# Where the low halves of two weight units are summed: VectorE or an accumulating DMA

## The chip, the cores and the metric

The kernel runs on one core of a Trainium2 chip. The metric is the device time of one execution in microseconds (us); the time given for a kernel is the median of its runs. A profile is one more execution, taken with the hardware profiler; its span runs from the first to the last instruction.

## The reference

Two layers of a transformer-like trunk are run for 640 tokens (128 context tokens and 512 latent tokens) with 1024 features, all in float32. Each layer has a mixer (a recurrent unit, neighbourhood attention, differential attention) and then a channel mixer, which is where the change lies:

```python
def conv_ffn(h, p):
    u = dwconv_centred(h @ p['ffn_up'], p['ffn_conv_w'], p['ffn_conv_b'])
    val, gate = jnp.split(u, 2, axis=-1)
    return (jax.nn.gelu(gate) * val) @ p['ffn_down']
```

`ffn_up` is 1024 x 5632 and `ffn_down` 2816 x 1024 in each layer; the 2816 middle features are handled as 22 tiles of 128, each with a value half and a gate half.

## The kernel before, in words

**Three products for one.** A float32 operand is held as a high half in the fast type fp32r and a low half, the rest. A product is formed as high x high + low x high + high x low, three matrix instructions for each. The split of a weight unit is made by `unit` (L366): ScalarE copies the source into the high half (`wh`, through `copy`, L110), and VectorE subtracts that from the source into the low half (`wl`, through `sub`, L117). Both halves live in a ring of four buffers of 128 x 1024 elements for each half.

**Seven products for eight.** For tiles 3 to 21 of the 22, class `Up` forms the 2 x 2 block product of weights and tokens with seven products (Strassen and Winograd's scheme) in place of eight. `up_weights` (L552) prepares the weights of one tile: two DMAs on SyncE's queue load them (`up_load`, L549), VectorE writes a sum `s1` (L556, tile `pT`) and an edit of the first half of the loaded buffer in place; then come unit y (first half of the buffer), unit x (second half, as loaded), two more in-place edits, which overwrite the second half, unit z (the edited second half) and a small unit `ws`, split from `s1`. y, x and z have 128 x 1024 elements each. Every edit and split is on VectorE or ScalarE; GpSimd does nothing in this stage.

**Order of the work.** One pass of the loop in `ffn` handles one tile. TensorE's products for the tile, in the order of the trace and in its names: p2 (`s<-h`, unit x), part of a `ffn_down` product (`m<-act`, unit of `rawd`), p4 (`t<-tx`, x), p6 (`m<-tx`, z), then p1 of the next tile (`m<-h`, y), p5 (`m<-h,ws`), p7 of the next tile (`t<-tx`, y), p3 (`m<-h`, z), and three more `ffn_down` parts (`s<-act`, `m<-act`, `s<-act`). Each is 12 matrix instructions on 320 columns. The order in which each engine's instructions stand is fixed ahead of time by a planner, which takes the ready instruction of the best priority by its own estimates of durations; it can set a matrix instruction ahead of another that it expects to wait. On the chip each engine runs its list in that order and waits where an operand is late. A ring buffer goes to whichever unit comes next when it falls free.

p6, p5 and p3 are added into one PSUM bank in turn, with a copy out by ScalarE (`raw<-m`, `u<-m`) between them: p5 may not start before the copy behind p6 is done.

Of the kernel before, what the change touches and what calls it, by code (L numbers as in the profile page):

```python
# [10 lines left out]
F32 = mybir.dt.float32  # L11
FR = mybir.dt.float32r
I32 = mybir.dt.int32
AF = mybir.ActivationFunctionType
OP = mybir.AluOpType
# [53 lines left out]
def trunk_kernel(ctx: ExitStack, tc: tile.TileContext, A, O):  # L69
    nc = tc.nc  # L70
# [19 lines left out]
    def pT_tile(w):  # L90
        return gen.tile([P, T], F32, tag="pT", name="pT", bufs=2)[:, :w]
# [16 lines left out]
    def copy(eng, out, in_):  # L108
        if eng == "a":
            return nc.scalar.activation(out, in_, AF.Copy)  # L110
        elif eng == "v":
            nc.vector.tensor_copy(out, in_)
        else:
            nc.gpsimd.tensor_copy(out, in_)

    def sub(out, a, b, eng=None):
        (eng or nc.vector).tensor_tensor(out, a, b, op=OP.subtract)  # L117
# [35 lines left out]
    for t in range(NT):  # L153
        src = A["x_prompt"] if t == 0 else A["x_sample"]
# [211 lines left out]
    split = []  # L366

    def unit(src, k, eng="a", home=None):
        wh, wl = [home(f"w{x}") if home else ring.tile([P, 1024], FR, tag=f"w{x}", name=f"w{x}") for x in "hl"]
        n = int(np.prod(src.shape[1:]))  # L370
        wh, wl = [w[:, :n].rearrange("p (k c) -> p k c", k=k) for w in (wh, wl)]
        split.append(copy(eng, wh, src))
        sub(wl, src, wh.bitcast(F32))
        return wh, wl

    def lx_groups(h, units, *jh):
# [33 lines left out]
    with tc.tile_pool(name="pro", bufs=1) as pro:  # L410
        raws = lx_load(0, [0])
        units = [unit(raws[j], 8) for j in range(2)]
        ws = [pro.tile([P, 2048], F32, name=f"pro{k}") for k in range(KD - 1)]
        ws = [[w[:, i * 512:i * 512 + 512] for i in range(4)] for w in ws]
# [30 lines left out]
        for part in range(4):  # L445
# [8 lines left out]
            if part < 3:  # L454
                for hf in range(2):
                    norm_apply(xt, 0, 0, hf + 2, h, range(part * 2 + 2, part * 2 + 4))
        units.append(unit(raws[2], 8))

    def attn_consts(l, mix):
# [33 lines left out]
    def wsplit(raw, nk, ncol, by_k=False, home=None):  # L493
        raw = raw[:, :nk * ncol].rearrange("p (k c) -> p k c", k=nk)
        kk, cc = (nk // 2, ncol) if by_k else (nk, ncol // 2)
        parts = [unit(raw[:, i * kk:i * kk + kk] if by_k else raw[:, :, i * cc:i * cc + cc], kk, home=home)
                 for i in range(2)]

        def get(k, c0, c1):
            i = k // kk if by_k else c0 // cc  # L500
            k, o = (k - i * kk, 0) if by_k else (k, i * cc)
            return tuple(w[:, k, c0 - o:c1 - o] for w in parts[i])
        return get
# [41 lines left out]
    def up_load(l, i):  # L545
        raw = raw_tile("up")
        w3 = raw.rearrange("p (k c) -> p k c", k=8)
        for v in range(2):
            nc.sync.dma_start(w3[:, :, v * P:v * P + P], dram(A["ffn_up"], l * D * 2 * FF + v * FF + i * P,  # L549
                                                            ((2 * FF, P), (P * 2 * FF, 8), (1, P))))  # L550
        return w3

    def up_weights(l, i):
        w3 = up_load(l, i)
        s1 = pT_tile(512).rearrange("p (k c) -> p k c", k=4)
        nc.vector.tensor_tensor(s1, w3[:, :4, P:], w3[:, 4:, P:], op=OP.add)  # L556
        yield
        sub(w3[:, :4, P:], w3[:, :4, :P], w3[:, :4, P:])
        y = unit(w3[:, :4], 4)
        yield y  # L560
        x = unit(w3[:, 4:], 4)
        yield x
        sub(w3[:, 4:, P:], s1, w3[:, :4, :P])
        sub(w3[:, 4:, :P], w3[:, 4:, :P], w3[:, 4:, P:])
        z = unit(w3[:, 4:], 4)
        yield z
        w = ring.tile([P, 1024], FR, tag="ws", name="ws", bufs=1)
        wh, wl = [w[:, i:i + 512].rearrange("p (k c) -> p k c", k=4) for i in (0, 512)]
        copy("a", wh, s1)
        sub(wl, s1, wh.bitcast(F32))  # L570
        yield wh, wl

    def up_begin(l, i):
        g = up_weights(l, i)
        next(g)
        return g, next(g), next(g)
# [923 lines left out]
```

## Time and profile before

| | us |
|---|---|
| median of 3 runs (1621.7 to 1622.51) | 1622.3 |
| the profiled execution | 1619.05 |
| its span, first to last instruction | 1616.9 |

Shares of the span in the profile are averages over many stages; the rows below take the stages apart. PE is TensorE's matrix instructions, PEld its weight loads, which overlap them; DVE is VectorE, ACT ScalarE, POOL GpSimd, SP SyncE. In a timeline row the first number is the start in us and the second the duration; a bracket holds the idle time of the engine just before, and what ended it. Matrix instructions are pipelined: one begins about every 0.147 us while its row says 0.31.

### The profile page before, as it was taken

The page shows a single profiled execution, that of the slowest core. Times are in us where ns is not written, and L with a number is a line of the kernel's source. Part 1 is how long each engine was busy: PE and PEld are TensorE (multiplying, and loading weights), DVE is VectorE, ACT ScalarE, POOL GpSimd, SP SyncE. Part 2 cuts the span into 40 slices and gives each one's busy share as a digit, 9 for nine tenths or more (in the row PEclk, how much of TensorE's full clock was granted, in tenths as well). Part 3 has the DMA queues.
Part 4 walks back from the last instruction along what each step waited for, and adds up shares of the span by engine and source line. Part 5 has one row for each costly group of instructions (what it writes and reads, how often), then busy time and mean ns, then how long its engine had stood idle before and what let it go on. Part 6 is the DMA issues. An engine that isn't in the chain of part 4 may idle for free.

```text
span 1616.9 us, 28663 instructions
## 1 busy us (share of the span) xinstructions
PE 1575.7 (97%) x11183; PEld 1466.1 (91%) x11183; DVE 1327.0 (82%) x2885; ACT 921.0 (57%) x1689; POOL 112.4 (7%) x98
## 2 busy tenths in 40 slices
PE   6999999999999999999999899999999999999998
PEld 5877688799999999999998777888999999999998
DVE  5886758888999888888897775778889998888884
ACT  5865647746655445445468656576475544544451
POOL 0310300102000000000012211000100000000000
PEclk8999999999999999999999999999999999999999
DMA  9566541131444333222244563221222332222221
GB/s 327 178 195 223 128 142 37 69 106 37 140 127 138 106 92 92 84 76 72 89 143 145 175 211 92 95 86 46 79 63 72 91 103 79 79 80 79 72 72 66
DMA packets 208070, 177.30 MB, mean 110 GB/s; under 512 B 47575, under 2 KB 197311, under 8 KB 201791
## 3 DMA queue, kind: packets, MB, share of 16 engines
q1 hardware_dynamic: 207934, 175.48, 35.3%
q8 instruction: 88, 1.44, 0.4%
q14 instruction: 48, 0.39, 0.1%
HBM read 165.12 MB, written 10.34 MB: 109 GB/s over the span
## 4 chain that ended last, share of the span: by engine, by line
PE 86%; DVE 6%; DMA 3%; ACT 2%; issue 2%; SPq 1%; POOL 0%; ACTq 0%; DVEq 0%; POOLq 0%
PE m L277 6%; PE m L279 6%; PE m L278 6%; PE m L1238 6%; PE m L1239 6%; PE m L1240 6%; PE s L278 4%; PE s L279 4%; PE s L277 4%; PE m L268 4%; PE m L270 4%; PE m L269 4%; PE t L1240 3%; PE t L1238 3%; PE t L1239 3%; PE t L934 2%
## 5 line engine op out<-in xcount | busy, mean ns | idle before, releaser
L117 DVE TENSOR_TENSOR wl<-up,wh 128x1024 fp32r<-128x1024 f32 x126 | 156.3, 1245 | 38.1 <-ACT wh L110 37.1
L1296 DVE SCALAR_TENSOR_TENSOR u<-raw,vec,u 128x127 f32<-128x127 f32 x352 | 175.8, 546 | 0.8 <-ACT u L1290 0.8
L110 ACT ACTIVATE wh<-up 128x1024 fp32r<-128x1024 f32 x126 | 132.2, 1051 | 77.7 <-PE t L1240 43.2
L268 PE MATMUL m<-wh,h 128*128 128x256 f32 x480 | 140.3, 292 | 0.0
L270 PE MATMUL m<-wh,h 128*128 128x256 f32 x480 | 138.3, 288 | 0.0
L269 PE MATMUL m<-wl,h 128*128 128x256 f32 x480 | 137.8, 287 | 0.0
L277 PE MATMUL m<-act,wh 128*128 128x320 f32 (+2 forms) x376 | 116.7, 311 | 0.0
L278 PE MATMUL m<-act,wl 128*128 128x320 f32 (+2 forms) x376 | 116.6, 310 | 0.0
L277 PE MATMUL s<-act,wh 128*128 128x320 f32 (+2 forms) x376 | 116.4, 310 | 0.0
L278 PE MATMUL s<-act,wl 128*128 128x320 f32 (+2 forms) x376 | 116.3, 309 | 0.0
L279 PE MATMUL s<-act,wh 128*128 128x320 f32 (+2 forms) x376 | 116.3, 309 | 0.0
L279 PE MATMUL m<-act,wh 128*128 128x320 f32 (+2 forms) x376 | 116.1, 310 | 0.0
L279 PE MATMUL m<-h,wh 128*128 128x320 f32 (+2 forms) x352 | 111.2, 319 | 3.0 <-DVE h L117 1.9
L277 PE MATMUL m<-h,wh 128*128 128x320 f32 (+2 forms) x352 | 112.5, 321 | 0.3 <-DVE xt L531 0.2
L278 PE MATMUL m<-h,wl 128*128 128x320 f32 (+2 forms) x352 | 111.3, 317 | 0.0
L531 DVE SCALAR_TENSOR_TENSOR xt<-m,mod,xt 128x128 f32<-128x128 f32 (+3 forms) x236 | 95.8, 432 | 14.2 <-PE m L279 13.1
L268 PEld LDWEIGHTS m<-wh,h 128*128 128x128 f32 x480 | 91.8, 191 | 14.5 <-issue 11.2
L269 PEld LDWEIGHTS m<-wl,h 128*128 128x128 f32 x480 | 91.9, 191 | 3.1 <-issue 2.9
L1238 PE MATMUL m<-h,wh 128*128 128x320 f32 x304 | 94.5, 311 | 0.0
L110 ACT ACTIVATE raw<-m 128x320 f32<-128x320 f32 x126 | 54.5, 432 | 70.1 <-PE m L1240 60.3
L270 PEld LDWEIGHTS m<-wh,h 128*128 128x128 f32 x480 | 91.7, 191 | 2.9 <-issue 2.4
L1240 PE MATMUL t<-tx,wh 128*128 128x320 f32 x304 | 94.2, 310 | 0.0
(364 smaller groups left out, 5072.1 us busy)
## 6 DMA issues: line engine op xcount, KB each, us to landing
up<-in_ffn_up_dram SPq DMA_DIRECT2D x88, 512.0 KB
adaw<-in_ada_w_dram SPq DMA_DIRECT2D x40, 1024.0 KB
w<-in_w_in_dram SPq DMA_DIRECT2D x16, 1024.0 KB
rawd<-in_ffn_down_dram SPq DMA_DIRECT2D x24, 512.0 KB
pro<-in_ada_w_dram SPq DMA_DIRECT2D x30, 256.0 KB
w<-in_w_out_dram SPq DMA_DIRECT2D x8, 768.0 KB
rawd<-in_ffn_down_dram SPq DMA_DIRECT2D x16, 384.0 KB
xd<-xt SPq DMA_DIRECT2D x4, 1280.0 KB
```

The costliest lines, as they stand in the source:

```text
L110: return nc.scalar.activation(out, in_, AF.Copy)
L117: (eng or nc.vector).tensor_tensor(out, a, b, op=OP.subtract)
L268: nc.tensor.matmul(out, st[0], mv[0], start=(i == 0), stop=False)
L269: nc.tensor.matmul(out, st[0], mv[1], start=False, stop=False)
L270: nc.tensor.matmul(out, st[1], mv[0], start=False, stop=(i == n - 1))
L277: nc.tensor.matmul(out, a[0], b[0], start=(k == total[0]), stop=False)
L278: nc.tensor.matmul(out, a[1], b[0], start=False, stop=False)
L279: last = nc.tensor.matmul(out, a[0], b[1], start=False, stop=(k == total[-1]))
L1238: nc.tensor.matmul(ps, st[0], mv[0], start=first and k == 0, stop=False, skip_group_check=chk)
L1239: nc.tensor.matmul(ps, st[1], mv[0], start=False, stop=False, skip_group_check=chk)
L1240: nc.tensor.matmul(ps, st[0], mv[1], start=False, stop=last and k == 3, skip_group_check=chk)
L1296: nc.vector.scalar_tensor_tensor(u[:, oa:ob], r[:, oa + sft:ob + sft], w, u[:, oa:ob], op0=OP.mult, op1=OP.add)
```

## The change

In `unit`, a new mode "d" has ScalarE write the high half as before, then a second ScalarE instruction writes the negated source, in fp32r, into the low half, and a DMA issued from GpSimd's queue adds the source onto it. `up_weights` uses the mode for y and x; z and `ws` stay as they are, and so do all units outside `up_weights`.

```diff
-        split.append(copy(eng, wh, src))
-        sub(wl, src, wh.bitcast(F32))
+        split.append(copy("a" if eng == "d" else eng, wh, src))
+        if eng == "d":
+            nc.scalar.activation(wl, src, AF.Copy, scale=-1.0)
+            nc.gpsimd.dma_start(wl, src, accum_op=OP.add)
+        else:
+            sub(wl, src, wh.bitcast(F32))
...
-        y = unit(w3[:, :4], 4)
+        y = unit(w3[:, :4], 4, "d")
         yield y
-        x = unit(w3[:, 4:], 4)
+        x = unit(w3[:, 4:], 4, "d")
         yield x
```

## Rows read from the trace of the kernel before

**Rows 1.** The page, part 1: busy us, share of span, instructions.
```profile
PE 1575.7 (97%) x11183; PEld 1466.1 (91%) x11183; DVE 1327.0 (82%) x2885; ACT 921.0 (57%) x1689; POOL 112.4 (7%) x98
```

**Rows 2.** Windows, both seven-product stages: us, busy by engine, clock, DMA share, GB/s.
```profile
424.00:800.00 376.00, 376.00 (x2563) 366.43 (x2562) 328.15 (x589) 189.69 (x280) 0.00 (x0) 1.00 0.35 104
...
1217.00:1576.00 359.00, 359.00 (x2444) 358.26 (x2444) 317.17 (x545) 183.53 (x274) 0.00 (x0) 1.00 0.28 82
```

**Rows 3.** Timeline of TensorE, one tile and the next.
```profile
567.51 0.31 PE L279 MATMUL s<-act,wh 128*128 128x320 f32 x1
...
574.69 0.31 PE L1238 MATMUL m<-h,wh 128*128 128x320 f32 x1
574.84 0.31 PE L1239 MATMUL m<-h,wl 128*128 128x320 f32 x1
...
576.45 0.31 PE L1238 MATMUL m<-h,ws 128*128 128x320 f32 x1
...
587.16 0.31 PE L1239 MATMUL s<-h,wl 128*128 128x320 f32 x1
...
593.76 0.31 PE L1239 MATMUL m<-h,wl 128*128 128x320 f32 x1
```

**Rows 4.** Waits of TensorE's weight loads, 1217 to 1576: us, times, longest.
```profile
PEld m L1238 <- ACT raw L110: 0.4, 2, 0.2
PEld m L278 <- DVE wl L117: 0.2, 1, 0.2
```

**Rows 5.** Tile `pT` (the sum `s1`): its instructions; what VectorE waited for.
```profile
L556 DVE TENSOR_TENSOR pT<-up x38: 682/686/962, 384.4 to 1527.9; 128x512 f32<-128x512 f32 x38
...
  DMA up<-in_ffn_up_dram: 3.7, 7
```

**Rows 6.** Groups of VectorE, 1217 to 1576.
```profile
L117 DVE TENSOR_TENSOR wl<-up,wh 128x1024 fp32r<-128x1024 f32 x55 | 67.1, 1224 | 20.3 <-ACT wh L110 20.0
```

**Rows 7.** The page, part 5: ScalarE's copies of weight units.
```profile
L110 ACT ACTIVATE wh<-up 128x1024 fp32r<-128x1024 f32 x126 | 132.2, 1051 | 77.7 <-PE t L1240 43.2
```

**Rows 8.** Windows of 1 us, end of one tile's weight loads.
```profile
588.00:589.00 1.00, 1.00 (x9) 1.00 (x8) 1.00 (x3) 0.43 (x1) 0.00 (x0) 1.00 1.02 333
589.00:590.00 1.00, 1.00 (x9) 1.00 (x8) 1.00 (x2) 0.00 (x0) 0.00 (x0) 1.00 0.26 74
```

**Rows 9.** Timeline of ScalarE, the same tiles.
```profile
568.09 1.04 ACT L110 ACTIVATE wh<-up 128x1024 fp32r<-128x1024 f32 x1
...
572.82 0.74 ACT L110 ACTIVATE act<-u 128x640 fp32r<-128x640 f32 x1 [3.68 <-DVE u L1301]
573.46 1.04 ACT L110 ACTIVATE wh<-up 128x1024 fp32r<-128x1024 f32 x1
574.89 0.44 ACT L110 ACTIVATE raw<-m 128x320 f32<-128x320 f32 x1 [0.39 <-PE m L1240]
...
587.39 1.04 ACT L110 ACTIVATE wh<-up 128x1024 fp32r<-128x1024 f32 x1
```

**Rows 10.** Timeline of VectorE, the same tiles.
```profile
569.17 1.23 DVE L117 TENSOR_TENSOR wl<-up,wh 128x1024 fp32r<-128x1024 f32 x1
...
574.76 1.22 DVE L117 TENSOR_TENSOR wl<-up,wh 128x1024 fp32r<-128x1024 f32 x1
...
576.30 0.69 DVE L117 TENSOR_TENSOR up<-pT,up 128x512 f32<-128x512 f32 x1
```

**Rows 11.** Timeline of SyncE's queue: a load of 1 MB alone.
```profile
109.85 0.38 SPq L359 DMA_DIRECT2D w<-in_w_in_dram  x1
```

**Rows 12.** Windows of 1 us behind that load; the last two numbers are DMA.
```profile
111.00:112.00 1.00, 1.00 (x8) 0.85 (x8) 1.00 (x3) 1.00 (x3) 0.34 (x1) 1.00 0.76 223
...
113.00:114.00 1.00, 0.05 (x1) 0.06 (x1) 0.89 (x1) 0.02 (x1) 0.21 (x1) 1.00 1.08 377
114.00:115.00 1.00, 1.00 (x8) 1.00 (x9) 0.00 (x0) 0.51 (x2) 0.00 (x0) 1.00 0.23 66
```

**Rows 13.** Groups of GpSimd: its additions on 128 x 256.
```profile
L971 POOL TENSOR_TENSOR naset<-naset,cst 128x256 f32<-128x256 f32 x24 | 22.9, 964 | 140.2 <-DMA naset<-t2d 128.9 <-PE s L983 6.2 <-DVE p L941 2.1
```

## The prediction

> **What bounds the kernel now.** I read the page's first part, then the busy times by stage, then the timeline of one tile, then TensorE's waits. The page shows TensorE at 97% and VectorE at 82% of the span [rows 1]. That is an average; the change acts only in the two stages in which `Up` runs. There TensorE is busy 376.00 of 376 us and 359.00 of 359 us [rows 2]. Its records overlap, so this alone could hide stalls; the count settles it: 2444 matrix instructions in 359 us are 0.1469 us each, the spacing at which they start back to back (574.69 to 574.84) [rows 2, 3]. The weight loads wait in that stage for two releases of 0.2 us by ScalarE and one by VectorE [rows 4]. So TensorE sets the time in both stages and waits for nothing. VectorE at 328.15 of 376 us (87%) is the next engine, ScalarE has half its time free, GpSimd is idle [rows 2]. VectorE's load costs nothing as it stands.
>
> **What is removed and added.** One sum `s1` is made per tile, and there are 38 [rows 5], so 76 units change. VectorE loses 76 subtractions of 1.224 us [rows 6], 93 us, some 2.45 us per tile of about 19.4 us. ScalarE gains 76 negated copies. I price them like the copies of the same shape, 1.051 us [rows 7]: 80 us, which takes it from 51% to about 61% of these stages. The direct worth of both is nothing: TensorE has no wait that the 93 us could shorten, and ScalarE stays below two thirds. GpSimd's queue gets 76 DMAs of 512 KB; nothing else is on it in these stages. The transfer engines are 28 to 35% busy there [rows 2]; 76 DMAs at the 4.3 us that I find below are 327 us of 735, much but not all, and the weight loads are not late by it: a tile's loads end near 589.3 [rows 8], and y of that tile is split a whole pass later.
>
> What can cost time is the latency. The low half was ready 1.22 us after the subtraction began; now it is ready after a copy on ScalarE and a DMA, and TensorE waits for it.
>
> **Unit y.** Its first use is p1. TensorE starts p1 at 574.69 and wants the low half with the second instruction, 574.84 [rows 3]. The only low half of this kind written shortly before is the one at 569.17, whose high half was copied at 568.09 [rows 9, 10]. The copy could not stand much earlier: the ring buffer that it takes falls free when the last `ffn_down` part ends at about 567.66 (start 567.51) [rows 3]. So the chain is: buffer free, copy 1.05, negated copy 1.05, DMA, p1. From 568.09 the two copies end at 570.19, and 574.84 - 570.19 = 4.65 us is left for the DMA. In the shorter pass, where one `ffn_down` part has nine instructions, it is 587.39 + 2.10 = 589.49 to 593.76, 4.27 us [rows 3, 9].
>
> No accumulating DMA and no DMA of GpSimd is in the trace. The nearest row is a load of 1 MB alone: issued at 109.85, its bytes flow until about 114.2 (377 GB/s in the slice from 113, 66 in the next), so 4.3 us [rows 11, 12]. An accumulating DMA of 512 KB reads 512 KB of source and, I take it, 512 KB of destination: the same 1 MB of reading. *Lower bound:* a plain copy of half the bytes: about 1.1 us until bytes flow and 0.52 MB at 380 GB/s, 2.5 us. *Upper bound:* all three passes over the engines one after the other, 1.57 MB at the 333 GB/s of the weight loads [rows 8], 4.7 us, with the 1.1 us start, and one GpSimd instruction of 0.96 us [rows 13] for what GpSimd does to build it: 6.8 us. I take 4.3 us, the row that moves the same amount, and keep 2.5 and 6.8. Against 4.65 us the y of an ordinary pass is in time by 0.35 us; against 4.27 it is late by 0.03 us in the few short passes. Sum: zero to 0.3 us in all.
>
> The Trainium skill prices such a DMA in "DMA: Bandwidth & Descriptors", section "Anatomy of one DMA — SWDGE (gpsimd) path": about 2.0 us fixed and the bytes at 436 GB/s. By that page a plain copy of 512 KB is an estimated 3.2 us. The same page ("Rules for kernel authors") says that the accumulate reads its destination and writes it later; if that reading costs as much again, the estimate is 4.4 us. By the first nothing would be late; by the second y would be late by 0.1 us in the short passes only. No run here shows either yet.
>
> If y were late, something stands behind it. The planner fixes the order by its own estimate. Three `ffn_down` parts, 36 instructions of 0.147 us or 5.3 us, come later in the pass and need neither y nor z; they can be put ahead of p1. The planner's view of loads looks cautious: the 38 sums are the first to read a tile's load, and VectorE waited for it 7 times, 3.7 us in all [rows 5]. So if the planner expects 5 us, TensorE fills the gap with these parts; only where the chip is slower than the planner thinks does TensorE stand still.
>
> **Unit x.** Its copy starts at 573.46 and its low half is first read at 587.16 [rows 3, 9]. After two copies (575.56) 11.6 us are left, above the upper bound. But two edits overwrite x's source; now the first follows the subtraction at 576.30 [rows 10], then it must wait for the DMA, to about 575.56 + 4.3 = 579.9. It stands in VectorE's list, and what is behind it waits too: p5's addition, the split of `ws`, and the additions that empty the PSUM banks of the `ffn_down` parts. With an honest estimate the planner moves those ahead. Without one VectorE stops for 3.6 us a pass, of which it has saved 2.45 and had 2.5 free (13% of 19.4). I take zero, with the loss bounded by the same 36 passes times about 1 us.
>
> **ScalarE's order.** The copy that frees p6's bank starts at 574.89, ends at 575.33, and p5 starts at 576.45 [rows 3, 9]: 1.1 us of slack. The negated copy of x comes ready just there (after 573.46 + 1.05). Put ahead, it takes 1.05 us of the 1.1. With the copy into `act` (0.74 us, 572.82) also ahead p5 would be 0.7 us late.
>
> **The sum** against the profiled execution: span 1616.9 + 0 = 1616.9, with the 2.15 us around it 1619.05, 3.25 us under the median. On the median's scale it is 1622.3 + 0.2 = 1622.5 us.
>
> **Rivals.**
>
> *No change (0.45).* As worked out: the transfers fit their gaps or the planner fills them. For it: TensorE has no wait to shorten, and 5.3 us of work is at hand. Its own range is 1619 to 1625.5.
>
> *y arrives late at p1 (0.32), slower.* Place: TensorE's second instruction of p1, waiting for GpSimd's DMA. It decides once the DMA takes over 4.65 us (4.27 in short passes) and more than the planner expects. The first tile of each stage is prepared early, so 36 passes pay. Midway between 4.3 and the 6.8 us bound, at 5.55, each pays 0.9 us: 32 us, 1655 us. At the bound it is 2.15 us, 77 us, 1700 us. For it: the gap is hardly longer than my estimate, and nothing of the trace shows GpSimd's share. Against it: the parts that can fill.
>
> *VectorE or ScalarE held up in order (0.13), slower.* The edit behind x's DMA, or the copy of p6's bank behind two others. At 0.3 us a pass, 36 passes: 11 us, 1633 us. Against it: VectorE gains more slack than it had.
>
> *Faster (0.10).* VectorE is at 87%, and with 93 us less its evacuations come sooner. Against it: only weight-load gaps remain, 376.00 - 366.43 = 9.6 us in the first stage and 0.7 in the second [rows 2], and the former are shared with other matrix work that has nothing to do with VectorE. If half goes: 1617.5 us. That the change does not do what it says ends here or at no change: VectorE's freed time would become idle time.
>
> **How the numbers follow.** A difference of 0.2%, 3.2 us, is about what a measurement of this kernel tells from none. No change 0.45, slower 0.32 + 0.13 = 0.45, faster 0.10; the likeliest single case gives 1622.5 us. The range runs from 1617, near the faster case, to 1670, past the priced case of y and under its bound; a tenth is left out above and a little below.
>
> **What would show it.** Right: in the changed profile the stages of `Up` still have about 0.147 us per matrix instruction, no wait of TensorE for GpSimd's DMA, VectorE at some 75%, ScalarE at some 61% there, and DMAs that land some 4.3 us after the negated copy. p1 later in the order than p6, with `ffn_down` parts between, would show the planner filling. Wrong: TensorE's waits name the low half `wl` and the DMA, or `raw`; the passes lengthen by a like amount each; or the DMAs take over 6.8 us, so that the order cannot cover them.

## The result and the profile after

The changed kernel takes 1668.0 us (median of 4 runs, 1665.0 to 1669.5) against 1622.4 us of the kernel before on the same chip: a ratio of 1.0285, 95% interval 1.0273 to 1.0298. It is slower, by 45.6 us. The likeliest case, no change at 1622.5 us, fell. The time lies inside the stated range, near its upper end of 1670, where the priced case of "y arrives late at p1" (1655 us) and that of the held VectorE (1633 us) would stand if they added up.

The span of the profiled execution is 1663.1 us, 46.2 more than before. Cut where p2 of the first and of the last tile of the loop begins, the stage of layer 0 takes 378.3 us instead of 353.7 and that of layer 1 366.2 instead of 343.7: 24.6 and 22.5 us. The rest of the kernel is 0.9 us shorter. All of the loss is in the two stages.

From the page of the kernel after, to be held against [rows 1, 7] (busy us, share and instructions; a queue's packets, MB and share; groups with busy us, mean ns and the idle time before them; issues with us to landing):

```profile
PE 1592.2 (96%) x11183; PEld 1469.1 (88%) x11183; DVE 1240.7 (75%) x2809; ACT 993.4 (60%) x1765; POOL 179.5 (11%) x174
...
q0 software_dynamic: 10944, 39.85, 12.7%
...
L375 POOL DMA_DIRECT2D wl<-up x76 | 66.1, 870 | 732.8 <-DVE raw L1255 310.8
...
L1243 PE MATMUL m<-h,wl 128*128 128x320 f32 x304 | 98.0, 322 | 21.0 <-DMA wl<-up 20.8
...
L117 DVE TENSOR_TENSOR up<-pT,up 128x512 f32<-128x512 f32 x38 | 26.3, 693 | 117.8 <-DMA wl<-up 117.8
L374 ACT ACTIVATE wl<-up 128x1024 fp32r<-128x1024 f32 x76 | 80.1, 1054 | 55.4 <-PE t L1243 39.2
...
wl<-up POOLq DMA_DIRECT2D x76, 512.0 KB, 4.8
```

VectorE lost 86 us of work and ScalarE gained 72 over the whole span; the 76 negated copies alone are 80.1 us. What is new is idle time behind `DMA wl<-up`, the new transfers: 20.8 us of TensorE ahead of line 1243, p1's second instruction, and 117.8 us of VectorE ahead of the edit that overwrites x's source.

The two stages in windows wide enough for the longer passes (as [rows 2]):

```profile
424.00:840.00 416.00, 400.31 (x2674) 384.75 (x2674) 300.18 (x592) 229.90 (x327) 32.74 (x38) 0.99 0.57 142
...
1240.00:1610.00 370.00, 355.05 (x2368) 350.13 (x2368) 267.92 (x495) 211.53 (x301) 31.22 (x36) 0.99 0.54 130
```

TensorE, busy all of the time before, has 15.7 and 15.0 us of holes in its records, and the spacing in the second window is 370 / 2368 = 0.156 us where it was 0.1469. The transfer engines went from 35 and 28% to 57 and 54%.

The waits of the kernel after, of TensorE's weight loads, VectorE and SyncE's queue (us in total, times, longest), where [rows 4], of the stage of layer 1, had three waits of 0.2 us and none for a DMA:

```profile
PEld m L1243 <- DMA wl<-up: 28.5, 29, 2.8
...
DVE up L117 <- DMA wl<-up: 117.8, 36, 6.6
...
SPq L195 <- DMA wl<-up: 46.9, 5, 14.6
```

L195 issues the loads of the next layer's conditioning weights. In the kernel before they waited for VectorE at that point, here from 400 to 600 us:

```profile
SPq L195 <- DVE wl L117: 53.1, 4, 18.1
```

All waits of L195 in that stretch add up to 78.3 us before and to 101.0 us after.

**A steady pass.** The timeline of the kernel after around one p1 (start, duration; bracket: idle time before and what ended it), ScalarE, GpSimd, then TensorE, to be held against [rows 3, 9]:

```profile
609.41 0.74 ACT L1303 ACTIVATE u<-u 128x640 f32<-128x640 f32 x1 [2.30 <-DVE u L1300]
610.06 1.04 ACT L110 ACTIVATE wh<-up 128x1024 fp32r<-128x1024 f32 x1
611.01 1.04 ACT L374 ACTIVATE wl<-up 128x1024 fp32r<-128x1024 f32 x1
...
612.46 0.89 POOL L375 DMA_DIRECT2D wl<-up  x1 [14.83 <-DVE raw L1255]
...
616.27 0.31 PE L1242 MATMUL m<-h,wh 128*128 128x320 f32 x1
617.06 0.42 PE L1243 MATMUL m<-h,wl 128*128 128x320 f32 x1 [0.47 <-DMA wl<-up]
```

The negated copy ends at 612.05, GpSimd starts 0.41 us later, and p1's second instruction begins at 617.06, 0.79 us after the first instead of 0.15. p1 still stands directly behind p6: the planner moved no part in between. This is one of the shorter passes, with nine `ffn_down` instructions ahead of p1; it took 20.1 us instead of 19.4. In most of this layer's steady passes with twelve, the second instruction comes 0.3 to 0.4 us after the first, and they take 19.6 to 19.7 us.

**An early pass of layer 0.** SyncE also loads the next layer's conditioning weights here, 1 MB each, in turn with the tiles' `ffn_up` weights in the same two buffers. The events of the kernel after on GpSimd, SyncE, TensorE and VectorE, in that order, and then 2-us windows (busy by engine, granted clock, DMA share, GB/s):

```profile
444.04 0.86 POOL L375 DMA_DIRECT2D wl<-up  x1 [25.24 <-ACT wl L374]
445.99 0.88 POOL L375 DMA_DIRECT2D wl<-up  x1 [1.10 <-ACT wl L374]
...
444.41 0.99 SPq L553 DMA_DIRECT2D up<-in_ffn_up_dram  x2
...
450.33 0.41 PE L1243 MATMUL m<-h,wl 128*128 128x320 f32 x1 [2.35 <-DMA wl<-up]
...
452.09 0.47 PE L1242 MATMUL m<-h,wh 128*128 128x320 f32 x1
452.36 0.47 PE L1243 MATMUL m<-h,wl 128*128 128x320 f32 x1
...
454.89 0.69 DVE L560 TENSOR_TENSOR pT<-up 128x512 f32<-128x512 f32 x1 [6.62 <-DMA up<-in_ffn_up_dram]
```

```profile
448.00:450.00 2.00, 0.00 (x0) 0.00 (x0) 0.28 (x1) 0.00 (x0) 0.00 (x0) 1.00 1.01 206
450.00:452.00 2.00, 1.67 (x8) 1.68 (x9) 0.00 (x0) 0.00 (x0) 0.00 (x0) 0.74 1.17 328
452.00:454.00 2.00, 2.00 (x10) 2.00 (x9) 0.00 (x0) 0.77 (x2) 0.00 (x0) 0.50 1.12 226
454.00:456.00 2.00, 2.00 (x14) 2.00 (x14) 1.11 (x2) 0.44 (x1) 0.00 (x0) 0.90 0.28 52
```

y's and x's DMAs and the load of a tile flow at once; the transfer engines are full for the 6 us from 448, p1 waits until 6.3 us after y's issue, and VectorE stands 6.62 us for a load that was issued 10.5 us earlier. After this stall of 2.35 us the granted clock of TensorE falls to 0.50, the 1.2 GHz level, and the stall costs more than its length: from 451.0 to 454.2 instructions start 0.267 us apart (452.09 to 452.36) instead of 0.147, which takes some 1.4 us more for the twelve that fit there. The first seven passes of layer 0 took 159.8 us instead of 139.0: 20.8 of that stage's 24.6 us.

### The profile page after: what moved, and what is told of

Same layout as the page of the kernel before. It is cut to its first block, busy times and chain, and to the rows that moved or that the text cites. A ratio compares the mean times of both kernels' runs of the same rounds, so it can differ in the third digit from the quotient of the medians.

```text
span 1663.1 us, 29017 instructions
## 1 busy us (share of the span) xinstructions
PE 1592.2 (96%) x11183; PEld 1469.1 (88%) x11183; DVE 1240.7 (75%) x2809; ACT 993.4 (60%) x1765; POOL 179.5 (11%) x174
## 4 chain that ended last, share of the span: by engine, by line
PE 66%; DMA 10%; issue 10%; DVE 9%; ACT 3%; SPq 1%; POOL 0%; POOLq 0%; DVEq 0%; ACTq 0%
DMA wl<-up 7%; PE m L277 5%; PE m L279 5%; PE m L278 5%; PE m L1243 4%; PE m L1244 4%; PE m L1242 4%; PE s L278 4%; PE s L277 3%; PE s L279 3%; PE m L268 3%; PE m L270 3%; PE m L269 3%; PE t L938 2%; DMA up<-in_ffn_up_dram 2%
## 5 line engine op out<-in xcount | busy, mean ns | idle before, releaser
L375 POOL DMA_DIRECT2D wl<-up x76 | 66.1, 870 | 732.8 <-DVE raw L1255 310.8
L1243 PE MATMUL m<-h,wl 128*128 128x320 f32 x304 | 98.0, 322 | 21.0 <-DMA wl<-up 20.8
L117 DVE TENSOR_TENSOR up<-pT,up 128x512 f32<-128x512 f32 x38 | 26.3, 693 | 117.8 <-DMA wl<-up 117.8
L374 ACT ACTIVATE wl<-up 128x1024 fp32r<-128x1024 f32 x76 | 80.1, 1054 | 55.4 <-PE t L1243 39.2
L268 PEld LDWEIGHTS m<-wh,h 128*128 128x128 f32 x480 | 91.7, 191 | 14.5 <-issue 12.1
```

Source lines behind the costliest of these rows:

```text
L268: nc.tensor.matmul(out, st[0], mv[0], start=(i == 0), stop=False)
L374: nc.scalar.activation(wl, src, AF.Copy, scale=-1.0)
L1243: nc.tensor.matmul(ps, st[1], mv[0], start=False, stop=False, skip_group_check=chk)
```

## The experiments

Passes are counted from one tile's start of p2 to the next; before, a steady one takes 19.4 us. "Before" is the kernel before, run beside the experiment.

**One unit each.** y alone, then x alone, in mode "d":

```diff
-        x = unit(w3[:, 4:], 4, "d")
+        x = unit(w3[:, 4:], 4)
```

> Only unit y takes its low half from the accumulating DMA; x is subtracted on VectorE as before. Theory A (TensorE waits for y's low half at p1, 0.3 to 0.9 us in each of 36 passes): most of the 45.6 us stays, 1645 to 1668 us, and TensorE's waits still name the DMA at p1. Theory B (VectorE stands still behind x's DMA, and what it delays is what costs): 1622 to 1630 us. The two acting on each other: between, 1635 to 1650.

1642.4 us against 1621.0 (ratio 1.0123, interval 1.0108 to 1.0138): 21.4 us, the mixed case of the expectation. TensorE's weight loads still name y's DMA:

```profile
PEld m L1243 <- DMA wl<-up: 18.7, 25, 3.7
```

```diff
-        y = unit(w3[:, :4], 4, "d")
+        y = unit(w3[:, :4], 4)
```

> Only unit x takes its low half from the accumulating DMA; y is subtracted on VectorE as before. Theory A: 1621 to 1627 us, TensorE has no wait for the DMA although VectorE still waits some 3 us a pass before it overwrites x's source. Theory B: 1645 to 1668 us.

1636.6 us (1.0087, 1.0072 to 1.0102): 15.6 us, which missed both theories, though TensorE has no wait for the DMA, as theory A said. The two together are 37.0 of the 45.6 us, and some 8.6 come only when both are there. They lose in different places. y alone costs 11.5 us in layer 0 and 9.8 in layer 1, the first pass of each stage and then 0.2 to 1.3 us in most passes. x alone costs 15.9 us in layer 0, all of it in the first seven passes, and 2.5 in layer 1, nearly all in the first pass; its steady passes are 19.4 us to the last. Yet VectorE waits in every one of them: waits of x alone, whole span, and its window from 600 to 780, then the same window of the kernel before:

```profile
DVE up L117 <- DMA wl<-up: 80.0, 37, 4.5
```

```profile
600.00:780.00 180.00, 180.00 (x1229) 180.00 (x1228) 144.32 (x257) 94.66 (x139) 7.79 (x9) 1.00 0.43 112
```

```profile
600.00:780.00 180.00, 180.00 (x1229) 180.00 (x1228) 154.72 (x265) 90.07 (x133) 0.00 (x0) 1.00 0.29 84
```

TensorE is busy 180.00 of 180 us, with the 1229 instructions of the kernel before. So some 2 us of VectorE a pass (80.0 / 37) are free to give, as long as y is not late as well.

**What the engines' loads are worth.** The negated copy on ScalarE stays, and VectorE adds the source, so that the units are as early as before but for one more copy:

```diff
-            nc.gpsimd.dma_start(wl, src, accum_op=OP.add)
+            nc.vector.tensor_tensor(wl, wl.bitcast(F32), src, op=OP.add)
```

> Both units keep the negated copy on ScalarE, but VectorE adds the source onto it, in place of the DMA. Theories A and B (the latency of the DMA): 1621 to 1627 us, since y's low half is ready 1.2 us after the negated copy. Theory C (the 80 us of ScalarE's negated copies cost the time): 1645 us or more.

1621.5 against 1621.0 us, ratio 1.0000 (0.9989 to 1.0011). Page part 1 of this kernel:

```profile
PE 1578.8 (97%) x11183; PEld 1468.3 (91%) x11183; DVE 1328.7 (82%) x2885; ACT 989.9 (61%) x1765; POOL 111.4 (7%) x98
```

ScalarE carries the whole 80 us more, at 61% of the span, and the time is that of before. The loss comes with the DMA, then, and not with the negated copies. VectorE keeps its load in this kernel, so what its relief is worth is not tested here.

**What the accumulation costs.** The same DMA without adding; the low half then holds the source, so this part of the computation is changed:

```diff
-            nc.gpsimd.dma_start(wl, src, accum_op=OP.add)
+            nc.gpsimd.dma_start(wl, src)
```

> As the changed kernel, but GpSimd's DMA copies the source into the low half and does not add it (the low half then holds the source: that part of the computation is changed). If the accumulating itself makes the DMA long (two reads, some 2.8 us of the transfer engines for 512 KB), a plain copy should need about half of them and land in some 3.4 us in place of 4.8: y is in time, 1622 to 1635 us. If the cost is GpSimd's queue and the fixed latency, landing stays at 4.5 us or more and the time at 1655 us or more.

1633.4 us against 1620.8 (1.0073, 1.0054 to 1.0091). Three lines of this kernel's page, for the three of the kernel after above:

```profile
q0 software_dynamic: 10944, 39.85, 6.9%
...
L375 POOL DMA_DIRECT2D wl<-up x76 | 40.5, 532 | 724.4 <-DVE raw L1255 298.5
...
wl<-up POOLq DMA_DIRECT2D x76, 512.0 KB, 2.9
```

For the same packets the accumulating DMA holds the 16 engines 0.127 x 1663.1 / 76 = 2.78 us, the copy 0.069 x 1630.4 / 76 = 1.48 (the factor is each kernel's span). It lands in 4.8 us at the median instead of 2.9, and takes GpSimd 870 ns instead of 532 to issue. With 1.9 us less, every steady pass is back at 19.4 us, and 12.6 us remain, 9.8 of them in the first seven passes of layer 0 and 2.5 in the first two of layer 1. Even the copy costs time at the start; that the loads there are the reason was not tested for it.

**Giving y more lead.** Three kernels: the negated copy and its DMA ahead of the copy to the high half; one `ffn_down` part ahead of p1, by hand, where the planner left it behind; and both.

```diff
-        split.append(copy("a" if eng == "d" else eng, wh, src))
         if eng == "d":
             nc.scalar.activation(wl, src, AF.Copy, scale=-1.0)
             nc.gpsimd.dma_start(wl, src, accum_op=OP.add)
+        split.append(copy("a" if eng == "d" else eng, wh, src))
+        if eng == "d":
+            pass
         else:
             sub(wl, src, wh.bitcast(F32))
```

> As the changed kernel, but the negated copy and the DMA are issued ahead of the copy into the high half, so that the DMA of y starts about 0.95 us earlier. Theory A: nearly all of the stall at p1 (0.35 us in ordinary passes, 0.73 in short ones) is gone, 1623 to 1638 us. Theory B: x's DMA already starts as early as it can, 1655 to 1668 us.

1649.4 us against 1621.0 (1.0169, 1.0152 to 1.0186): 0.95 us of lead takes back about 17 us of the loss, between the two theories. The steady passes are mostly back at 19.4 us and the stage of layer 1 falls from 366.2 to 353.8 us, but the first seven passes of layer 0 stay at 159.6.

```diff
             if nxt:
+                next(more, None)
                 nxt.p1()
```

> As the changed kernel, but one more ffn_down part (12 instructions, 1.77 us) is put ahead of p1 in the program, so that y has that much more time. Theory A (p1 waits 0.3 to 2.8 us for y): the waits at p1 fall from some 25 us to under 6, and in the second layer the stage goes from 366 us to 344 to 352; the whole 1640 to 1650 us, since the first layer's early passes keep their loss. If the waits at p1 are only where TensorE stands while something else is late, they reappear elsewhere and the time stays above 1660 us.

1651.1 us against 1620.8 (1.0188, 1.0173 to 1.0203). Past the seventh pass of layer 0 and the second of layer 1, no pass is over 0.2 us longer than before, and the steady ones take 19.4 to 19.5 us: the part fills the gap once it is put there. The first passes are no better (26.5 and 26.2 us), and the first seven of layer 0 take 164.0 us. So the time came out a little over what I had expected, as did the stage of layer 1 (354.3 us, with 344 to 352 expected) and the waits at p1 (9.2 us, below, with under 6 expected).

> After with both leads for y: the negated copy and the DMA ahead of the copy to the high half, and one ffn_down part ahead of p1. Theory (two separate losses: y late at p1 in the steady passes of both layers, and the first seven passes of layer 0, where the DMAs share buffers and engines with the 1 MB loads): the steady loss is gone, passes of 19.4 to 19.5 us in both layers, and the early 20 us and a few us in the first pass of each stage stay: 1640 to 1648 us. Rival A (each lead alone already gave all that a lead can give): no better than the order change alone, 1648 to 1652 us. Rival B (the early passes too are y late at p1, and 2.7 us of lead cover it): 1624 to 1636 us.

1643.3 us against 1621.7 (1.0131, 1.0109 to 1.0152), as the first theory had it. Waits of TensorE's weight loads, first with both leads, then of the kernel with a part first alone:

```profile
PEld m L278 <- DVE wl L117: 10.7, 8, 2.1
PEld m L1243 <- DMA wl<-up: 5.3, 4, 2.0
```

```profile
PEld m L278 <- DVE wl L117: 9.8, 7, 2.0
PEld m L1243 <- DMA wl<-up: 9.2, 4, 3.1
```

29 waits for y's DMA have become 4. What now ends most of TensorE's waits is the split of an `ffn_down` unit, read by line 278, which comes late in VectorE's list: in one of the early passes it stands behind the held edit (5.3 us), in four behind the next tile's `s1`, which waits 1.3 to 2.4 us for its load from `ffn_up`. Layer 0 is 19.9 us longer than before, 19.5 of it in the first seven passes; layer 1 is 5.2 longer, 4.8 of it in the first pass.

**Both leads, y alone.** Which of the two units still costs:

```diff
-        x = unit(w3[:, 4:], 4, "d")
+        x = unit(w3[:, 4:], 4)
```

> Both leads, but only unit y takes the DMA; x is subtracted by VectorE as before. Theory (y costs time only where it is late at p1, and the leads cover it in all but a few early passes): 1621 to 1628 us, steady passes of 19.4 us, no wait of TensorE for the DMA outside the first seven passes of layer 0. Rival (the DMA costs time by itself, through the engines or VectorE's edits behind it, whatever the lead): near y alone without the leads, 1635 to 1642 us. None of them is under the kernel before by more than 2 us, since TensorE has no idle time there.

1625.4 us against 1621.7 (1.0028, 1.0017 to 1.0038): 3.7 us. With lead, y's DMA is nearly free; what both leads leave, 21.6 us, is x's for the most part. One of TensorE's waits for the DMA, 1.5 us, stands in the first pass of layer 1, where none was expected. The waits of its weight loads:

```profile
PEld m L1243 <- DMA wl<-up: 5.0, 3, 2.0
...
PEld m L278 <- DVE wl L117: 0.6, 1, 0.6
```

This is the best form of the change that I found, and it is still slower than the kernel before.

**The loads of the early passes.** The two calls that put the conditioning weights' loads between the tiles are taken out, so that this work runs behind the loop: in the kernel before, in x alone, and in the kernel with both leads.

```diff
             old.conv(*act_tile(), i == 21)
-            next(ada, None)
```

> The kernel before, but the loads and small products of the next layer's modulation (adaw) are no longer interleaved with the first layer's passes; they all come after the loop. It is the reference for the next run alone. 1620 to 1660 us: the eight loads of 1 MB are no longer hidden, but the early passes shorten.

> Only x by the accumulating DMA, and the modulation's loads after the loop as in the run beside it. If x's 15.6 us come from the first layer's early passes, in which adaw takes turns with the weights in the two load buffers and the transfer engines, the difference to the run beside it falls to 0 to 5 us. If VectorE's standing behind x's DMA costs by itself, it stays at 12 us or more.

> The same two leads, and the 1 MB loads of the next layer's conditioning weights taken out of the tile loop and run behind it, as in the kernel before with the same shift (1633.8 us). Theory (the early loss comes from sharing with these loads): 1635 to 1642 us, 1 to 8 us over that kernel, with the first seven passes of layer 0 near 125 to 132 us. Rival (the early loss has nothing to do with the loads): 20 us or more over it, 1653 us and above.

The control takes 1633.8 us against 1620.8. x alone takes 1640.5, 6.7 over its control instead of 15.6, a little more than I had expected. Its first seven passes in layer 0 take 133.2 us, 2.9 more than the control's 130.3, and 2.3 of that is the first pass; in layer 1 the first pass loses 2.4. So the collision with those loads is over half of what x alone loses. With both leads it is 1647.5 us against 1621.7 (1.0153, 1.0136 to 1.0170): 25.9 us, 12.8 more than the control's own 13.0, where without the shift it was 21.6. This missed the 1 to 8 us of the theory as well as the 20 of the rival: the first seven passes take 141.7 us, 11.4 more than the control's. What is left there stands in two places: the first pass of each stage (23.2 us where the control has 17.9, in both layers), and the fifth pass of layer 0, 25.0 instead of 19.4, where GpSimd's DMAs run beside the stage's own loads (1 MB of `ffn_up` issued at 506.86, `ffn_down` at 508.46). Two of this kernel's windows in that pass:

```profile
513.00:517.00 4.00, 2.83 (x17) 2.13 (x15) 3.26 (x6) 1.65 (x3) 0.88 (x1) 1.00 1.08 250
517.00:521.00 4.00, 3.42 (x17) 3.42 (x18) 0.86 (x2) 0.44 (x1) 0.00 (x0) 0.73 0.48 94
```

The engines are full, the DMAs issued here take 7.0 to 8.5 us to land, and the clock falls again. So the conditioning weights seem to be only one of the loads with which the DMAs collide. That the stage's own loads make the rest I read from this pass alone; no run took them away.

## Where the prediction was right and where it failed, by its own steps

*The range: it held, and the mechanism of the chosen value did not.* The sum put the loss at 0.2 us; the range reached 1670 us only because it was drawn past the priced case of y. That 1668.0 lies in it is owed to that case and to the loss by x's DMA, which the sum had put at zero.

*What bounds the kernel: right.* TensorE set the time and waited for nothing, so neither the 93 us taken from VectorE nor the 80 us given to ScalarE should change anything. For ScalarE the runs show it (1.0000 with VectorE adding); for VectorE the steady passes of x alone do, which stay at 19.4 us with 144.32 us of VectorE's work in 180 us instead of 154.72. For the same reason "faster" was never there. ScalarE's order, feared at p6's bank, cost nothing either.

*Unit y, the DMA's price: the step that failed first.* I took 4.3 us, the row of a 1 MB load, against 4.65 us of room. The DMA takes 4.5 us at the least and 4.8 at the median, and 0.41 us pass between the end of the negated copy and GpSimd's start (0.30 to 0.42 over all 76). That hand-over was in no term of the chosen value. With 4.9 us y is late by 0.25 us against the 4.65 of an ordinary pass, and by 0.64 us against the 4.27 of a shorter one. The pass shown is of the shorter kind, and late by about that, 0.79 - 0.15 us. The bounds, 2.5 and 6.8 us, held the median, but beside loads the landing reached 9.2.

The copy's 2.9 us and the accumulation's 4.8 are some 10% either side of what I had worked out from the Trainium skill, "DMA: Bandwidth & Descriptors", section "Anatomy of one DMA — SWDGE (gpsimd) path": an estimated 3.2 us, and 4.4 if the reading of the destination costs as much again. That second assumption is close to what the engines show, 2.78 us against 1.48.

*"The planner fills": wrong.* I read its 3.7 us of waits for loads as caution and gave it 5 us of expected DMA. p1 did not move. The runs show that the work was at hand (a part put there by hand brings the passes to 19.4 or 19.5 us), so a missing part was not the reason. That the planner took the DMA for shorter than it is, or gave p1 the better priority all the same, is not settled: its figure was not looked at.

*Unit x, "I take zero": wrong at the beginning of each stage, right in the steady passes.* The edit did wait as worked out, and the steady passes paid nothing (19.4 us). But the first seven passes of layer 0 are not like the one that I took the times from. There the tile loads and the conditioning weights take turns in two buffers, and x's source must now be held until its DMA has read it: the loads of the conditioning weights wait 46.9 us for a DMA in 5 turns, and all their waits there grow from 78.3 to 101.0 us. They then start later, and flow together with the DMAs. I had written that "the weight loads are not late by it" from one steady tile.

*The rivals' sum.* The y rival had the place right, TensorE's second instruction of p1, and mis-sized it: 0.9 us in 36 passes, where y alone shows 0.2 to 1.3 in most and 21.4 us in all. The held VectorE was priced at 11 us; x alone cost 15.6. That they add up, and more, I had not weighed: they were given as alternatives. The remaining 8.6 us I read as a loop between them. By the stages of the profiles this excess stands in layer 1 alone: 22.5 us with both units, 9.8 and 2.5 with one; in layer 0 both cost 24.6 us, less than 11.5 and 15.9 together. The loop can be read in a pass of layer 1, from the timeline of the kernel after, first on VectorE and ScalarE at the end of the pass before it, then on ScalarE, GpSimd, TensorE and VectorE:

```profile
1395.78 0.69 DVE L117 TENSOR_TENSOR up<-pT,up 128x512 f32<-128x512 f32 x1 [5.30 <-DMA wl<-up]
...
1403.55 0.74 ACT L1303 ACTIVATE u<-u 128x640 f32<-128x640 f32 x1 [2.30 <-DVE u L1300]
1404.19 1.04 ACT L110 ACTIVATE wh<-up 128x1024 fp32r<-128x1024 f32 x1
1405.14 1.04 ACT L374 ACTIVATE wl<-up 128x1024 fp32r<-128x1024 f32 x1
...
1406.59 0.88 POOL L375 DMA_DIRECT2D wl<-up  x1 [16.65 <-DVE raw L1255]
1409.21 0.87 POOL L375 DMA_DIRECT2D wl<-up  x1 [1.74 <-ACT wl L374]
...
1411.19 0.41 PE L1243 MATMUL m<-h,wl 128*128 128x320 f32 x1 [2.41 <-DMA wl<-up]
...
1414.49 0.69 DVE L117 TENSOR_TENSOR up<-pT,up 128x512 f32<-128x512 f32 x1 [3.90 <-DMA wl<-up]
```

VectorE was held 5.3 us by the x of the pass before, what follows in its list (the convolution of the last tile) was late, ScalarE waited 2.3 us for that, and its copy of the next y came late in turn, at 1404.19, 2.3 us after p2 began, where in the pass shown above it was 0.4. y's DMA, issued late, is still flowing when x's is issued 2.6 us behind it; x lands late, and VectorE is held again, 3.9 us. Passes of 22.0 and 23.7 us stand in layer 1 of the kernel after, and in neither of the kernels with a single unit (their steady passes take 20.7 us at most). That each arrow is the cause of the next is read from the trace; what is shown by runs is that the excess needs both units, and that layer 1 loses 5.2 us instead of 22.5 when y has both leads.

The 45.6 us, then: about 21.4 from y late at p1, 15.6 from x's DMA holding VectorE and the loads at the beginning of the stages, 8.6 from both together. A part of it is the lower clock behind a long stall: in windows of 1 us over the two stages the granted clock falls four times in the kernel after, once each in y alone and in x alone, and never in the kernel before. What it lacks to 1.00 adds up to 6.8, 3.4 and 1.7 us. Not settled: how the 4.8 to 6.0 us of the first pass of each stage, which stay with both leads, divide between p1's wait, the held splits and the `ffn_down` part placed ahead of p1.

## What to carry to other kernels

Work moved from a busy engine to a DMA is free only where a deadline is far: compare the whole chain (producer's end to issuer's start, issue to landing, beside the busiest loads) with the room at the first reader, and count as a second deadline whatever overwrites the source. Where the engine that sets the time has no idle time, relief of another engine is worth nothing, and every new wait can only cost. Take the room from the first passes of a stage as well as from a steady one, and do not count on a planner to fill a gap without looking at the length that it plans with.

## What the runs showed of the hardware

- Adding in a DMA nearly doubles the transfer engines' time for the same 512 KB (2.78 us against 1.48) and the time to landing grows from 2.9 to 4.8 us; GpSimd's part grows from 0.53 to 0.87 us.
- GpSimd starts 0.30 to 0.42 us after the instruction on ScalarE that it waits for has ended (76 DMAs of the kernel after). Beside weight loads the landing of an accumulating DMA stretches to 9.2 us.
- A stall of 2.35 us was followed by three windows of 2 us at a granted clock of 0.74, 0.50 and 0.90; instructions then start 0.267 us apart instead of 0.147, so that the clock is part of a stall's price.
